# First layer's gate and up products as 2x2 blocks with seven block products

## The chip, the core and the metric

One NeuronCore of a Trainium2 chip runs the whole program. Its engines have queues of their own and work in order: TensorE (PE; weight loads are listed as PEld), VectorE (DVE), ScalarE (ACT), GpSimd (POOL) and SyncE (SP), which here only issues DMAs. The metric is the device time of one execution in microseconds (us).

## What is computed

Two layers work on 512 latent tokens x (1024 features) and 256 context tokens; the last layer keeps only the latents. Each layer has a mixer and then the FFN that the change is about, for both streams with the same weights:

```python
def swiglu(h, w_in, w_out):
    gu = h @ w_in
    return (jax.nn.silu(gu[..., :D_FF]) * gu[..., D_FF:]) @ w_out
...
x = x + mod_x[5] * swiglu(modulate(x, norm2_gain[i], mod_x[3], mod_x[4]), w_ffn_in[i], w_ffn_out[i])
...
cx = cx + mod_c[5] * swiglu(modulate(cx, norm2_gain[i], mod_c[3], mod_c[4]), w_ffn_in[i], w_ffn_out[i])
```

D_FF is 2816. All inputs are float32; `modulate` is an RMSNorm with a shift and a scale for each feature.

## The kernel before

Activations lie feature-major: 8 tiles of 128 features by the tokens, context first (columns 0 to 255), latents behind (256 to 767). Every operand of a product is split into a high part in the TensorE's float32r format and a low part, the exact rest, and a product is three matmuls: high by high, low weight by high, high weight by low (`gemm_step`, L290 to L292). A weight tile is loaded as 512 KB into one of four `rawp` buffers on SyncE's queue (`units`); ScalarE writes its high part (L272) and VectorE subtracts it for the low part (L273) into `hlp`, three buffers each.

`ffn` walks over the 22 hidden tiles j. For each it takes the gate and the up product of the context (256 columns) and of the latents (512 columns), all over 8 feature tiles k (`half`). ScalarE takes the silu of the gate out of PSUM (L883), VectorE multiplies it by the up product (L886), and `split_act` writes the high and low part of the hidden tile (L318, L319). After tiles 2, 6, 10, 14 and 18 a `chunk` takes the down products of the hidden tiles of the chunk before, two tiles in the first chunk and four in the others: for each of the 8 output tiles the context and then the latents, each in a PSUM bank of its own, and VectorE adds the result to the residual `X` (L854). The last four hidden tiles are in `finish0`.

Beside this runs `fill.tick()`, which once for each hidden tile advances the next layer's modulation vectors: a 512 KB tile of `w_mod`, two multiply-adds on VectorE (L222), and for the context two scalings on ScalarE (L219) and two adds on GpSimd (L220). The norm ahead of the FFN (`modulated`) takes the tokens' sums of squares on TensorE, a power on GpSimd (L329, `rs_n2c` and `rs_n2x`), spreads it over the partitions on TensorE and multiplies. The context's norm runs during the last products of the latents' mixer (`w_out`, names `po0x`), the latents' during the context's first gate and up products. In the latents' mixer the names are `g0x` and `b0x` for the gate and branch weights and products.

The order on each engine is that of the built program. The rows below name tiles without their numbers; the order's names keep them (`fa04` is the hidden tile 4 of layer 0).

## Time and profile before

| | |
|---|---|
| median of 3 runs | 2091.32 us (2089.07 to 2094.69) |
| span of the profiled execution | 2093.8 us |
| time of the profiled execution | no other than its span is listed |
| TensorE busy | 2024.5 us (97%) |
| VectorE, ScalarE, GpSimd busy | 1149.6, 744.4, 426.7 us (55, 36, 20%) |
| DMA, mean | 112 GB/s |

A busy time is the sum over an engine's instructions. Matmuls overlap in the records, so the start of one to the start of the next tells their rate, not their listed duration. PEclk is the clock that TensorE was granted, 1.00 for 2.4 GHz. An idle time in brackets stands in front of the instruction that ended it, with the instruction that released it.

### The profile page before, as it was taken

What the parts mean: (1) busy time and instruction counts of PE and PEld (TensorE: products, weight loads), DVE (VectorE), ACT (ScalarE), POOL (GpSimd) and SP (SyncE); (2) the same over time, 40 slices, a digit from 0 to 9 for tenths busy, and PEclk for the clock granted to TensorE, in tenths of its full rate; (3) what the DMA queues carried; (4) which work ended last, traced back from release to release, by engine and by line L of the source; (5) the groups of instructions that cost most, each with busy time, mean ns of one, the idle gap of its engine ahead of it and who ended that gap; (6) DMA issues with size and microseconds to landing.
All of it is one profiled execution on the core that took longest, in us unless ns stands there. A gap on an engine that the chain in (4) does not pass through costs nothing.

```text
span 2093.8 us, 28850 instructions
## 1 busy us (share of the span) xinstructions
PE 2024.5 (97%) x11615; PEld 1715.0 (82%) x11615; DVE 1149.6 (55%) x1765; ACT 744.4 (36%) x1231; POOL 426.7 (20%) x358
## 2 busy tenths in 40 slices
PE   7998999999899999999999999999999999999998
PEld 6988988777677888888888888787778788888887
DVE  4878638675666653434334335765756664344335
ACT  3655434344333422121313124443422333222223
POOL 4426302023664411000102013301111130000000
PEclk9999999999999999999999999999999999999999
DMA  9755633231544232222323223423336643333331
GB/s 294 207 165 153 202 101 101 63 104 51 159 153 131 81 91 73 88 81 71 91 61 101 71 71 89 109 61 90 88 102 211 178 132 91 100 95 97 101 92 59
DMA packets 326181, 233.46 MB, mean 112 GB/s; under 512 B 7648, under 2 KB 299664, under 8 KB 326048
## 3 DMA queue, kind: packets, MB, share of 16 engines
q1 hardware_dynamic: 322528, 226.78, 36.1%
q0 software_dynamic: 3280, 4.76, 1.1%
q8 instruction: 91, 1.49, 0.3%
q14 instruction: 42, 0.34, 0.0%
q10 hardware_dynamic: 240, 0.08, 0.0%
HBM read 225.30 MB, written 2.10 MB: 109 GB/s over the span
## 4 chain that ended last, share of the span: by engine, by line
PE 81%; DVE 10%; DMA 3%; issue 2%; ACT 2%; POOL 2%; ACTq 0%; SPq 0%; POOLq 0%; DVEq 0%
PE pg1x L290 2%; PE pg1x L291 2%; PE pg1x L292 2%; PE pfg0x L292 2%; PE pfg0x L291 2%; PE pfg0x L290 2%; PE pfg1x L292 2%; PE pfo0x L290 2%; PE pfo0x L291 2%; PE pfu1x L291 2%; PE pfo0x L292 2%; PE pfu1x L292 2%; PE pfu1x L290 2%; PE pfg1x L290 2%; PE pfg1x L291 2%
## 5 line engine op out<-in xcount | busy, mean ns | idle before, releaser
L220 POOL TENSOR_TENSOR mac<-mac,mq 128x512 f32<-128x512 f32 x84 | 124.4, 1481 | 296.9 <-ACT mq L219 293.0
L273 DVE TENSOR_TENSOR wl_fu<-raw_fu,wh_fu 128x1024 fp32r<-128x1024 f32 x44 | 63.6, 1446 | 153.9 <-ACT wh_fu L272 153.8
L222 DVE SCALAR_TENSOR_TENSOR mac<-wm,scv,mac 128x512 f32<-128x512 f32 x140 | 131.0, 936 | 13.4 <-DMA wm<-in_w_mod_dram 10.6
L272 ACT ACTIVATE wh_fg<-raw_fg 128x1024 fp32r<-128x1024 f32 x44 | 46.6, 1059 | 181.1 <-PE pfo0x L292 65.7
L273 DVE TENSOR_TENSOR wl_fo<-raw_fo,wh_fo 128x1024 fp32r<-128x1024 f32 x42 | 54.7, 1303 | 69.3 <-ACT wh_fo L272 69.3
L272 ACT ACTIVATE wh_fo<-raw_fo 128x1024 fp32r<-128x1024 f32 x42 | 44.4, 1058 | 122.4 <-issue 120.2
L291 PE MATMUL pg0x<-n1x0h,wl_g0x 128*128 128x512 f32 x192 | 77.2, 402 | 8.9 <-DVE wl_g0x L273 8.9
L290 PE MATMUL pg0x<-n1x0h,wh_g0x 128*128 128x512 f32 x192 | 77.1, 402 | 1.5 <-ACT wh_g0x L272 1.5
L290 PE MATMUL pg1x<-n1x1h,wh_g1x 128*128 128x512 f32 x192 | 76.4, 398 | 0.0
L292 PE MATMUL pg0x<-n1x0l,wh_g0x 128*128 128x512 f32 x192 | 76.4, 398 | 0.0
L291 PE MATMUL pg1x<-n1x1h,wl_g1x 128*128 128x512 f32 x192 | 75.8, 395 | 0.0
L292 PE MATMUL pg1x<-n1x1l,wh_g1x 128*128 128x512 f32 x192 | 75.8, 395 | 0.0
L329 POOL TENSOR_TENSOR rs_fin<-v_fin,half_neg 128x1 f32<-128x1 f32 x4 | 2.9, 721 | 355.3 <-DVE v_fin L327 355.3
L290 PE MATMUL pfg1x<-n2x1h,wh_fg 128*128 128x512 f32 (+1 forms) x184 | 70.5, 383 | 0.8 <-ACT n2x1h L359 0.8
L854 DVE SCALAR_TENSOR_TENSOR X<-pfo0x,modv,X 128x512 f32<-128x512 f32 x48 | 36.0, 750 | 64.0 <-PE pfo0x L292 64.0
L292 PE MATMUL pfg1x<-n2x1l,wh_fg 128*128 128x512 f32 (+1 forms) x184 | 70.5, 383 | 0.5 <-POOL n2x1l L360 0.3
L290 PE MATMUL pfu1x<-n2x1h,wh_fu 128*128 128x512 f32 (+1 forms) x184 | 70.0, 380 | 0.0
L291 PE MATMUL pfu1x<-n2x1h,wl_fu 128*128 128x512 f32 (+1 forms) x184 | 70.0, 380 | 0.0
L291 PE MATMUL pfg1x<-n2x1h,wl_fg 128*128 128x512 f32 (+1 forms) x184 | 69.9, 380 | 0.0
L292 PE MATMUL pfu1x<-n2x1l,wh_fu 128*128 128x512 f32 (+1 forms) x184 | 69.9, 380 | 0.0
L290 PE MATMUL pfo0x<-fa,wh_fo 128*128 128x512 f32 x176 | 69.0, 392 | 0.0
L291 PE MATMUL pfo0x<-fa,wl_fo 128*128 128x512 f32 x176 | 69.0, 392 | 0.0
(708 smaller groups left out, 6540.1 us busy)
## 6 DMA issues: line engine op xcount, KB each, us to landing
wm<-in_w_mod_dram SPq DMA_DIRECT2D x96, 512.0 KB, 4.0
raw_fg<-in_w_ffn_in_dram SPq DMA_DIRECT2D x44, 512.0 KB, 3.9
raw_fu<-in_w_ffn_in_dram SPq DMA_DIRECT2D x44, 512.0 KB, 3.8
raw_fo<-in_w_ffn_out_dram SPq DMA_DIRECT2D x42, 512.0 KB, 3.4
raw_g0c<-in_w_in_dram SPq DMA_DIRECT2D x24, 512.0 KB, 3.9
raw_g0x<-in_w_in_dram SPq DMA_DIRECT2D x24, 512.0 KB, 4.2
raw_g1x<-in_w_in_dram SPq DMA_DIRECT2D x24, 512.0 KB, 3.9
raw_wo0c<-in_w_out_dram SPq DMA_DIRECT2D x8, 512.0 KB, 4.0
```

The costliest lines, as they stand in the source:

```text
L220: G.tensor_tensor(a, a, q, ALU.add)
L222: V.scalar_tensor_tensor(a, raw[:, k, :], sck, a, ALU.mult, ALU.add)
L272: S.activation(wh, raw_ap, AF.Copy)
L273: (eng or V).tensor_tensor(wl, raw_ap, wh.bitcast(F32), ALU.subtract)
L290: T_.matmul(ps, wh, H, start=first, stop=False)
L291: T_.matmul(ps, wl, H, start=False, stop=False)
L292: T_.matmul(ps, wh, L, start=False, stop=last)
L329: G.tensor_tensor(rs, v, half_neg[:, :nb], ALU.pow)
L854: V.scalar_tensor_tensor(x, ps, modv[l][:, 40 + n, s.r:s.r + 1], x, ALU.mult, ALU.add)
```

## The change

The tokens of both streams together are cut into even and odd blocks of 128, two halves of 384 columns (one context block and two latent blocks each); the features into k tiles 0 to 3 and 4 to 7; the weights of a hidden tile into gate and up. With B for the four blocks of activations and A for the four of weights, a hidden tile's gate and up for both halves come from seven products of 4 k tiles by 384 columns instead of the eight that the blocks have: A11 B11, A12 B21, S1 T1, S2 T2, S3 T3, S4 B22, A22 T4 in the names of the code, where S and T are sums of weight blocks and of activation blocks. Sums of the products are made partly in PSUM, by products that are added into the same bank, and partly on VectorE.

The T sums are made once (`combine`); the S sums for every hidden tile from the loaded weights (`sums`, on GpSimd for tiles 0 and 1, on VectorE for the others), and the split is of S2, S1, S3, S4 and of A11, A12, A22. `Pipeline` prepares items (two products each, the last of a tile one; or two output tiles of a chunk) ahead of the products. The activations' norm is made by halves (`norm`); the last three `w_out` tiles of the latents are taken by halves, too, and half 0 is normed during the products of half 1 (`last_first`). In `chunk` the context and the latents share a PSUM tile (columns 512 to 767 and 0 to 511). Tiles 0 to 2 are interleaved at the start.

The raw buffers are five instead of four, for the whole kernel. Keys, attention and activation buffers lie in zones that are closed and opened by stage, so that the seven pairs of B and T blocks have room. Layer 1's FFN is as before.

```diff
-    rawp = ctx.enter_context(tc.tile_pool(name="rawp", bufs=4))
+    rawp = ctx.enter_context(tc.tile_pool(name="rawp", bufs=5))
     hlp = ctx.enter_context(tc.tile_pool(name="hlp", bufs=3))
-    act = ctx.enter_context(tc.tile_pool(name="act", bufs=11))
...
+    def zone(name, bufs, side="left"):
+        zones[name] = ExitStack()
+        return zones[name].enter_context(tc.tile_pool(name=name, bufs=bufs, side=side, reuse_waits="tile"))
...
+            ps = pmain(f"po{nm0}{n}_{a}{st.name}")[:, :st.T]
+            if st.odd is not None:
+                p3 = ps.rearrange("p (b t) -> p b t", t=P)
+                gemm(p3, ws[n], KT, *[[blocks(y, st.odd) for y in x] for x in yo])
+                x = blocks(X[:, n, s.cols], st.odd)
+                V.scalar_tensor_tensor(x, p3, modv[l][:, 16 + n, s.r:s.r + 1], x, ALU.mult, ALU.add)
+                q = t2(f"sq{st.name}{n}", st.T)
+                S.activation(q.rearrange("p (b t) -> p b t", t=P), x, AF.Square)
+                if n == KT - 1:
+                    acc.append(q)
+                else:
+                    t = blocks(acc[0], st.odd)
+                    G.tensor_tensor(t, t, q.rearrange("p (b t) -> p b t", t=P), ALU.add)
+                return
...
+        def split(self, nm, src, k0, k1):
+            c = self.C[nm]
+            S.activation(c[:, 0, k0:k1, :], src, AF.Copy)
+            V.tensor_tensor(c[:, 1, k0:k1, :], src, c[:, 0, k0:k1, :].bitcast(F32), ALU.subtract)
...
+        def norm(self, i, ss):
+            l = self.l
+            rs = rstd(ss(), 2, f"n2h{i}", D)
+            yield
+            rb = ps_s.tile([P, 1024], F32, tag="ps", name=f"ps_rbh{i}")[:, :HT]
...
+            for k in range(KT):
+                y = t[k // 4][:, k % 4, :]
+                V.tensor_tensor(y.rearrange("p (b t) -> p b t", t=P), blocks(X[:, k, :], i), rb.rearrange("p (b t) -> p b t", t=P), ALU.mult)
+                a, b = A2[l], modv[l]
+                S.activation(y[:, :P], y[:, :P], AF.Identity, bias=b[:, 24 + k, 1:2], scale=a[:, k, 1:2])
+                if k % 2:
+                    S.activation(y[:, P:], y[:, P:], AF.Identity, bias=b[:, 24 + k, 0:1], scale=a[:, k, 0:1])
+                else:
+                    V.tensor_scalar(y[:, P:], y[:, P:], a[:, k, 0:1], b[:, 24 + k, 0:1], ALU.mult, ALU.add)
+                yield
...
+            b11, b21, b12, b22 = self.t
+            T2 = self.fap.tile([P, 4, HT], F32, tag="fa", name="T2")
+            self.combo("T2")
+            for h in (slice(0, 2), slice(2, 4)):
+                V.tensor_tensor(b11[:, h], b12[:, h], b11[:, h], ALU.subtract)
+                V.tensor_tensor(T2[:, h], b22[:, h], b11[:, h], ALU.subtract)
+                self.split("T2", T2[:, h], h.start, h.stop)
+                yield
+            self.combo("T1")
+            self.split("T1", b11, 0, 4)
+            yield
+            V.tensor_tensor(b12, b22, b12, ALU.subtract)
+            self.combo("T3")
+            self.split("T3", b12, 0, 4)
+            yield
+            self.combo("B22")
+            self.split("B22", b22, 0, 4)
+            yield
+            V.tensor_tensor(b21, b21, T2, ALU.subtract)
+            self.combo("T4")
+            self.split("T4", b21, 0, 4)
...
+        def product(self, ps, w, k0, nm, first):
+            c = self.C[nm]
+            wh, wl = w
+            for k in range(4):
+                H, L = c[:, 0, k, :], c[:, 1, k, :]
+                T_.matmul(ps, wh[:, k0 + k, :], H, start=first and k == 0, stop=False, skip_group_check=True)
+                T_.matmul(ps, wl[:, k0 + k, :], H, start=False, stop=False, skip_group_check=True)
+                T_.matmul(ps, wh[:, k0 + k, :], L, start=False, stop=k == 3, skip_group_check=True)
...
+            def sums(which, eng=V):
+                g, u = d["g"], d["u"]
+                a11, a12, a21, a22 = g[:, 0:4, :], g[:, 4:8, :], u[:, 0:4, :], u[:, 4:8, :]
+                for x in which:
+                    if x == 3:
+                        d["S3"] = self.sp.tile([P, 4, P], F32, tag="S3", name=f"S3{j}")
+                        eng.tensor_tensor(d["S3"], a11, a21, ALU.subtract)
+                    elif x == 1:
+                        eng.tensor_tensor(a21, a21, a22, ALU.add)
+                    elif x == 2:
+                        eng.tensor_tensor(a11, a21, a11, ALU.subtract)
+                    else:
+                        eng.tensor_tensor(a12, a12, a11, ALU.subtract)
...
+            def prep_a():
+                load()
+                if early is None:
+                    sums((3, 1))
+                w = parts("sg", d["g"])
+                if early is None:
+                    sums((2,))
+                elif early < 2:
+                    sums((3, 1, 2, 4), G)
+                return w
+            def prep_b():
+                if early == 2:
+                    sums((3, 1, 2))
+                w = parts("sb", d["g"][:, 0:4, :], d["u"][:, 0:4, :])
+                if early in (None, 2):
+                    sums((4,))
+                return w
+            def prep_c():
+                return parts("sc", d["S3"], d["g"][:, 4:8, :])
+            def prep_d():
+                return parts("su", d["u"][:, 4:8, :])
...
+                self.product(d["P"], w, 0, "B11", True)
+                if early is None:
+                    evac_m()
+                elif early == 0:
+                    next(self.nx)
+                self.product(d["Q"], w, 4, "B21", True)
+                if early is None:
+                    evac_g()
+                else:
+                    self.late.append((evac_m, evac_g))
...
+            def evac_g():
+                d["g1"] = t2(f"g1{j}", HT)
+                V.tensor_tensor(d["g1"], d["Q"], d["m"], ALU.add)
+                S.activation(d["g1"], d["g1"], AF.Silu)
+            def run_b(w):
+                self.product(d["P"], w, 0, "T2", False)
+                d["m6"] = t2(f"m6{j}", HT)
+                S.activation(d["m6"], d["P"], AF.Copy)
+                d["R"] = bank(f"pR{j}") if early != 1 else ps_s.tile([P, 1024], F32, tag="ps", name=f"pR{j}")[:, :HT]
+                self.product(d["R"], w, 4, "T1", True)
+                d["m5"] = t2(f"m5{j}", HT)
+                S.activation(d["m5"], d["R"], AF.Copy)
+            def run_c(w):
+                self.product(d["P"], w, 0, "T3", False)
+                V.tensor_tensor(d["m5"], d["P"], d["m5"], ALU.add)
+                self.product(d["R"], w, 4, "B22", False)
+                V.tensor_tensor(d["m6"], d["R"], d["m6"], ALU.add)
+                S.activation(d["m6"], d["m6"], AF.Silu)
+            def run_d(w):
+                self.product(d["P"], w, 0, "T4", False)
+                H, L = A(j)
+                for i, (x, y) in enumerate(((d["P"], d["g1"]), (d["m5"], d["m6"]))):
+                    V.tensor_tensor(y, x, y, ALU.mult)
+                    y3 = y.rearrange("p (b t) -> p b t", t=P)
+                    S.activation(blocks(H, i), y3, AF.Copy)
+                    V.tensor_tensor(blocks(L, i), y3, blocks(H, i).bitcast(F32), ALU.subtract)
+                fill.tick()
...
+                def go(w, n=n):
+                    for i in range(2):
+                        ps = ps_s.tile([P, 1024], F32, tag="ps", name=f"pfo{l}{c0}{n + i}")
+                        for s in streams:
+                            o = 512 if s.r else 0
+                            down(s, n + i, [x[:, :, i * P:(i + 1) * P] for x in w], c0, m, ps[:, o:o + s.T])
...
+            p = [sv.pair(j, hidden, j) for j in range(3)]
+            for j, x in ((0, 0), (1, 0), (2, 0), (0, 1), (1, 1), (0, 2), (1, 2), (0, 3), (1, 3), (2, 1), (2, 2), (2, 3)):
+                yield p[j][x]
+                if j == 2 and x == 3:
+                    yield from chunk(0)
+            for j in range(3, NF):
+                yield from sv.pair(j, hidden)
+                if j in heads:
+                    yield from chunk(heads[heads.index(j) - 1])
...
+    seven = Seven(0)
+    def last_first(one, acc):
+        for i in range(2):
+            st = Stream(f"x{'eo'[i]}", CTX, 256, 0)
+            st.odd = i
+            part = [acc[0]]
+            acc0.append(part)
+            for n in range(KT - 3, KT):
+                one(n, st, part)
+                fill.tick()
+                if i:
+                    steps(n0, {KT - 3: 2, KT - 2: 4, KT - 1: 3}[n])
+            if i == 0:
+                close("att", "kkp")
+                seven.fap = zone("fap", 6, "right")
+                half_ss(0)
+                n0 = seven.norm(0, lambda: ssh[0])
+                next(n0)
...
+    pipe, end = ffn_seven(seven, [SC, SX], 0, finish0, [mod_steps(1, 0, 4)])
+    half_ss(1)
+    seven.nx = seven.norm(1, lambda: ssh[1])
+    for x, nm in enumerate(("B11", "B21")):
+        seven.combo(nm)
+        for h in (0, 2):
+            seven.split(nm, seven.t[x][:, h:h + 2, :], h, h + 2)
+        if x == 0:
+            pipe.fill(1)
+            next(seven.nx)
+    pipe.fill(2)
+    for _ in range(3):
+        pipe.step()
+    run(seven.nx)
+    cm = seven.combine()
+    seven.late[0][0]()
+    steps(cm, 2)
+    for m, _ in seven.late[1:]:
+        m()
+    for _, g in seven.late:
+        g()
+    run(cm)
+    while pipe.step():
+        pass
+    close("sp", "cbp")
+    open_act()
+    end()
```

GpSimd between the latents' mixer and the FFN, before: adds of squares (`sq_m0x`), the two streams' low parts (`n2c0l`, `n2x0l`) and the power for the latents (`rs_n2x`).

```order
L372 TENSOR_TENSOR sq_m0x0_6494<-sq_m0x0_6494,sq_m0x5_6702 128x512
L372 TENSOR_TENSOR sq_m0x0_6494<-sq_m0x0_6494,sq_m0x6_6742 128x512
L360 TENSOR_TENSOR n2c0l0_6544<-t_n2c05_6745,n2c0h0_6543 128x256
L329 TENSOR_TENSOR rs_n2x0_6845<-v_n2x0_6843,half_neg_97 128x4
L360 TENSOR_TENSOR n2c0l0_6544<-t_n2c07_6789,n2c0h0_6543 128x256
L360 TENSOR_TENSOR n2x0l0_6882<-t_n2x01_6889,n2x0h0_6880 128x512
L360 TENSOR_TENSOR n2x0l0_6882<-t_n2x03_6899,n2x0h0_6880 128x512
```

GpSimd at the same place now; `rs_n2h1` is the power for half 1, `raw_u0` and `raw_g0` the sums S1 and S2 in place.

```order
L859 TENSOR_TENSOR sq_m0x0_6509<-sq_m0x0_6509,sqxo6_6833 128x2x128
L1098 TENSOR_TENSOR S30_6910<-raw_g00_6902,raw_u00_6904 128x512
L1098 TENSOR_TENSOR S31_6932<-raw_g01_6924,raw_u01_6926 128x512
L1100 TENSOR_TENSOR raw_u00_6904<-raw_u00_6904 128x512
L1100 TENSOR_TENSOR raw_u01_6926<-raw_u01_6926 128x512
L1102 TENSOR_TENSOR raw_g00_6902<-raw_u00_6904,raw_g00_6902 128x512
L360 TENSOR_TENSOR rs_n2h1_6917<-v_n2h1_6915,half_neg_93 128x2
```

Five weight sums stand between the last add of squares and the power; the low parts have left the engine. On TensorE the matmuls that spread this power, `ps_rbh1`, stand ahead of the first product of tile 0, `pP0`.

VectorE during one hidden tile (4) before:

```order
L886 TENSOR_TENSOR sg0c4_7566<-sg0c4_7566,pfu0c4_7568 128x256
L319 TENSOR_TENSOR fa04_7528<-sg0c4_7566,fa04_7528 128x256
L273 TENSOR_TENSOR wl_fu02_384_7661<-raw_fu02_384_7658,wh_fu02_384_7660 128x1024
L886 TENSOR_TENSOR sg0x4_7621<-sg0x4_7621,pfu0x4_7623 128x512
L273 TENSOR_TENSOR wl_fg06_0_7800<-raw_fg06_0_7797,wh_fg06_0_7799 128x1024
L319 TENSOR_TENSOR fa04_7528<-sg0x4_7621,fa04_7528 128x512
```

VectorE during one hidden tile now; `m5`, `m6` and `g1` are sums of products, `raw_g05` and `raw_u05` hold the next tile's weights:

```order
L1104 TENSOR_TENSOR raw_g05_7777<-raw_g05_7777 128x512
L1190 TENSOR_TENSOR m64_7760<-pR4_7762,m64_7760 128x384
L1113 TENSOR_TENSOR wl_sb5_7817<-raw_g05_7777,wh_sb5_7816 128x512
L1113 TENSOR_TENSOR wl_sb5_7817<-raw_u05_7779,wh_sb5_7816 128x512
L1197 TENSOR_TENSOR m64_7760<-m54_7775,m64_7760 128x384
L1197 TENSOR_TENSOR g14_7741<-pP4_7713,g14_7741 128x384
L1113 TENSOR_TENSOR wl_sc5_7843<-S35_7781,wh_sc5_7842 128x512
L1200 TENSOR_TENSOR fa04_7835<-m64_7760,fa04_7835 128x3x128
L1113 TENSOR_TENSOR wl_sc5_7843<-raw_g05_7777,wh_sc5_7842 128x512
L1200 TENSOR_TENSOR fa04_7835<-g14_7741,fa04_7835 128x3x128
L1174 TENSOR_TENSOR g15_7876<-pS5_7849,m5_7862 128x384
L1113 TENSOR_TENSOR wl_su5_7880<-raw_u05_7779,wh_su5_7879 128x512
```

Six instructions for a tile became seventeen, and the next tile's sums and splits lie between this tile's sums out of PSUM; S3 and S1 of the tile after that stand further ahead.

VectorE at the start of a four-tile chunk before (down weights `fo`, hidden tile 6, first updates of `X`):

```order
L886 TENSOR_TENSOR sg0x6_7889<-sg0x6_7889,pfu0x6_7891 128x512
L273 TENSOR_TENSOR wl_fo02_512_8056<-raw_fo02_512_8053,wh_fo02_512_8055 128x1024
L319 TENSOR_TENSOR fa06_7796<-sg0x6_7889,fa06_7796 128x512
L854 SCALAR_TENSOR_TENSOR X_117<-pfo0c20_0_7935,modv0_134,X_117 128x256
L854 SCALAR_TENSOR_TENSOR X_117<-pfo0x20_0_7949,modv0_134,X_117 128x512
L854 SCALAR_TENSOR_TENSOR X_117<-pfo0c21_0_7963,modv0_134,X_117 128x256
```

VectorE at the start of the same chunk now:

```order
L1197 TENSOR_TENSOR g16_8033<-pP6_8005,g16_8033 128x384
L1197 TENSOR_TENSOR m66_8052<-m56_8067,m66_8052 128x384
L304 TENSOR_TENSOR wl_fo024_8140<-raw_fo024_8137,wh_fo024_8139 128x1024
L1200 TENSOR_TENSOR fa06_8120<-g16_8033,fa06_8120 128x3x128
L1200 TENSOR_TENSOR fa06_8120<-m66_8052,fa06_8120 128x3x128
L1221 SCALAR_TENSOR_TENSOR X_113<-pfo020_8143,modv0_141,X_113 128x256
L1221 SCALAR_TENSOR_TENSOR X_113<-pfo021_8170,modv0_141,X_113 128x256
L1098 TENSOR_TENSOR S37_8261<-raw_g07_8257,raw_u07_8259 128x512
L1100 TENSOR_TENSOR raw_u07_8259<-raw_u07_8259 128x512
L1098 TENSOR_TENSOR S38_8458<-raw_g08_8454,raw_u08_8456 128x512
L1100 TENSOR_TENSOR raw_u08_8456<-raw_u08_8456 128x512
L1221 SCALAR_TENSOR_TENSOR X_113<-pfo020_8143,modv0_141,X_113 128x512
```

Splits, both low halves of tile 6 and then the context's updates stand ahead, and S3 and S1 of tiles 7 and 8 ahead of the latents' updates.

## Rows read from the trace of the kernel before

**Rows 1.** Head of the page: span, then busy time of each engine.
```profile
span 2093.8 us, 28850 instructions
...
PE 2024.5 (97%) x11615; PEld 1715.0 (82%) x11615; DVE 1149.6 (55%) x1765; ACT 744.4 (36%) x1231; POOL 426.7 (20%) x358
```

**Rows 2.** Table by stretch, three stretches; first line gives the columns.
```profile
core 0: us, PE busy (x) PEld busy (x) DVE busy (x) ACT busy (x) POOL busy (x), PEclk, DMA share, GB/s
...
332.00:660.00 328.00, 308.29 (x1715) 243.42 (x1714) 222.23 (x360) 137.45 (x246) 127.65 (x94) 0.97 0.37 107
...
711.00:733.00 22.00, 21.16 (x139) 18.96 (x138) 14.81 (x27) 13.65 (x22) 9.52 (x7) 1.00 0.17 51
733.00:1238.00 505.00, 504.68 (x2939) 444.19 (x2938) 206.45 (x265) 120.81 (x174) 41.15 (x30) 1.00 0.27 81
```

**Rows 3.** Timeline of TensorE, gate products: start, duration, line, operation.
```profile
900.11 0.28 PE L291 MATMUL pfg0c<-n2c0h,wl_fg 128*128 128x256 f32 x1
...
900.83 0.28 PE L291 MATMUL pfg0c<-n2c0h,wl_fg 128*128 128x256 f32 x1
...
907.82 0.39 PE L290 MATMUL pfg0x<-n2x0h,wh_fg 128*128 128x512 f32 x1
...
908.50 0.39 PE L290 MATMUL pfg0x<-n2x0h,wh_fg 128*128 128x512 f32 x1
```

**Rows 4.** Groups by line and shape, VectorE, 660 to 1264 us: busy, mean ns.
```profile
L273 DVE TENSOR_TENSOR wl_fu<-raw_fu,wh_fu 128x1024 fp32r<-128x1024 f32 x22 | 36.6, 1666 | 89.2 <-ACT wh_fu L272 89.0
...
L273 DVE TENSOR_TENSOR wl_fg<-raw_fg,wh_fg 128x1024 fp32r<-128x1024 f32 x22 | 27.1, 1232 | 6.6 <-ACT wh_fg L272 6.6
L222 DVE SCALAR_TENSOR_TENSOR mac<-wm,scv,mac 128x512 f32<-128x512 f32 x28 | 22.0, 785 | 7.7 <-DMA wm<-in_w_mod_dram 7.1
L854 DVE SCALAR_TENSOR_TENSOR X<-pfo0c,modv,X 128x256 f32<-128x256 f32 x44 | 21.2, 481 | 12.7 <-PE pfo0c L292 12.5
L319 DVE TENSOR_TENSOR fa<-sg0x,fa 128x512 fp32r<-128x512 f32 x22 | 18.4, 834 | 0.0
L886 DVE TENSOR_TENSOR sg0x<-sg0x,pfu0x 128x512 f32<-128x512 f32 x22 | 15.1, 688 | 33.4 <-PE pfu0x L292 33.4
...
L886 DVE TENSOR_TENSOR sg0c<-sg0c,pfu0c 128x256 f32<-128x256 f32 x22 | 9.3, 421 | 53.6 <-PE pfu0c L292 53.6
...
L360 DVE TENSOR_TENSOR n2x0l<-t_n2x,n2x0h 128x512 fp32r<-128x512 f32 x4 | 2.8, 703 | 0.4 <-ACT n2x0h L359 0.4
```

**Rows 5.** Timeline around 762 us: GpSimd's row and VectorE's row.
```profile
761.22 2.67 POOL L220 TENSOR_TENSOR mac<-mac,mq 128x512 f32<-128x512 f32 x2 [16.50 <-ACT mq L219]
...
762.67 2.30 DVE L273 TENSOR_TENSOR wl_fo<-raw_fo,wh_fo 128x1024 fp32r<-128x1024 f32 x1 [6.87 <-ACT wh_fo L272]
```

**Rows 6.** Groups by line and shape, GpSimd, 660 to 1264 us.
```profile
L372 POOL TENSOR_TENSOR sq_m0x<-sq_m0x,sq_m0x 128x512 f32<-128x512 f32 x6 | 10.1, 1686 | 20.4 <-ACT sq_m0x L368 20.4
...
L360 POOL TENSOR_TENSOR n2x0l<-t_n2x,n2x0h 128x512 fp32r<-128x512 f32 x4 | 5.2, 1302 | 8.0 <-ACT n2x0h L359 8.0
...
L329 POOL TENSOR_TENSOR rs_n2c<-v_n2c,half_neg 128x2 f32<-128x2 f32 x1 | 0.7, 725 | 3.0 <-DVE v_n2c L327 3.0
```

**Rows 7.** Timeline of TensorE after a wait; in brackets the idle and its releaser.
```profile
641.18 0.79 PE L291 MATMUL pb0x<-y00xh,wl_b0x 128*128 128x512 f32 x1 [4.72 <-DVE wl_b0x L273]
...
645.61 0.60 PE L292 MATMUL pb0x<-y00xl,wh_b0x 128*128 128x512 f32 x1
646.04 0.40 PE L290 MATMUL pg0x<-n1x0h,wh_g0x 128*128 128x512 f32 x1
646.28 0.39 PE L291 MATMUL pg0x<-n1x0h,wl_g0x 128*128 128x512 f32 x1
```

**Rows 8.** Waits of TensorE and of ScalarE: total us, times, longest us.
```profile
PE pg0x L291 <- DVE wl_g0x L273: 8.9, 3, 4.8
...
ACT wh_g0x L272 <- DMA raw_g0x<-in_w_in_dram: 45.0, 10, 7.2
```

**Rows 9.** Timeline of VectorE ahead of that wait.
```profile
631.84 7.56 DVE L222 SCALAR_TENSOR_TENSOR mac<-wm,scv,mac 128x512 f32<-128x512 f32 x6
```

More of the change, by code (lines that the diff above doesn't have):

```diff
@@ L1 @@
 import math
+from collections import deque
 from contextlib import ExitStack
@@ L41, in __init__ @@
         self.NB = T // P
+        self.odd = None
     @property
@@ L941, in ffn, with __init__, fill, step @@
         chunk(heads[-1])
+    class Pipeline:
+        def __init__(self, items, depth):
+            self.items, self.depth, self.ready = iter(items), depth, deque()
+        def fill(self, n=None):
+            while len(self.ready) < (self.depth + 1 if n is None else n):
+                item = next(self.items, None)
+                if item is None:
+                    return
+                self.ready.append((item[1], item[0]()))
+        def step(self):
+            self.fill()
+            if not self.ready:
+                return False
+            do, w = self.ready.popleft()
+            do(w)
+            return True
```

139 lines of the change are left out of this document (128 added, 11 removed).

## The prediction

> **What bounds the kernel now.** I read the page's head first, then the table of stretches, then single rows. The profiled execution spans 2093.8 us and TensorE is busy for 2024.5 us of it; VectorE follows with 55% [rows 1]. The page shows no time outside the span, so the sum below is made against 2093.8 us; the median of the runs, 2091.32 us, is 2.5 us lower. The table by stretch shows where TensorE's idle time lies. In the first layer's FFN (733 to 1238 us) it idles 0.3 us of 505, and 0.84 us in the norm ahead of it (711 to 733). In the latents' mixer (332 to 660) it idles 19.7 of 328 us at a granted clock of 0.97 [rows 2]. So in the FFN a matmul saved is time saved, and nothing else is there to gain; any new wait of TensorE is a loss at full price. VectorE is busy 206 of the 505 us there, ScalarE 121: that is the room in which the scheme's sums must fit.
>
> **TensorE's work.** Three 512-column matmuls take from 907.82 to 908.50, one every 0.227 us; six of 256 columns from 900.11 to 900.83, one every 0.120 us [rows 3]. Both are 0.417 ns a column and 13 ns fixed, so the 384-column matmul, which the trace does not show at this depth, is taken at 0.173 us; its bounds are the two rows around it, and a break between them is not in sight. A hidden tile has 48 matmuls of each width (8 k x 3 x gate and up): 48 x 0.120 + 48 x 0.227 = 16.64 us. After: 7 products x 4 k x 3 = 84 x 0.173 = 14.56 us. 22 tiles: **-45.8 us**. The down products keep their 48 matmuls a tile. Three w_out tiles of the latents become two 256-column halves: 3 x 24 x (2 x 0.120 - 0.227) = **+1.0 us**.
> The Trainium skill ("TensorE: Matmul & The Clock Gate", Back-to-back issue gap) states N/2.4 + 2.5 ns; by it, as an estimate, a tile would save 1.95 us and all of them 42.9. The rows show some 11 ns more for each matmul than it states, so the measurement decides.
>
> **VectorE's work for a tile.** Before: two 1024-element splits (1.23 and 1.67), two products out of PSUM (0.42 and 0.69) and two low halves (the context's taken like its product, 0.42, the latents' 0.83), 5.3 us [rows 4]. After, 17 instructions: four sums of weights and five splits of 512 (0.70 each, the row of n2x0l: 6.3), one split of 1024 (1.23), and five sums or products out of PSUM and two low halves of 384, between the 0.42 of 256 and the 0.69 of 512 columns, so 0.555 each (3.9): 11.4 us. Two steps of a modulation sum add 2 x 0.785. That is 13.0 of the 14.56 us that TensorE needs for the tile; before, it was under half. It hides as long as nothing makes the queue wait. Two things do. S3 and S1 of a later tile stand in VectorE's queue ahead of this tile's sums and wait for a load (the order of VectorE shows it); and VectorE slows beside GpSimd: a 1024-element split took 2.30 us while GpSimd added two modulation rows (2.67 us) [rows 5], and wl_fg 1.23 in the mean [rows 4], so +1.07 us. GpSimd adds two rows a tile.
> The Trainium skill ("GPSIMD Engine Reference", Key points) says that GpSimd shares its SBUF interfaces with VectorE and contends with instructions that have two SBUF inputs. The trace agrees [rows 5], and the sums of weights and the splits are all such instructions, so this rule speaks against the change; its price in the sum is the 1.07 us of the row.
> With those 1.07 us a tile needs 14.1 us of VectorE, 0.5 less than TensorE. The 19 tiles in the steady rhythm then wait now and then; bounds are 0 and 1.2 us a tile (1.07 and a load that is late once more), and I take 0.4: **+8 us** (0 to 23), nearer to the margin that is left than to the full collision.
>
> **The transition.** Before, the latents' norm runs beside the context's first products, and TensorE idles 0.84 us in all [rows 2]. After, the first product needs both streams, and only half 0 is normed during w_out. I replayed the built program's order with the durations of the rows. (a) The factor of half 1 is a power on GpSimd, queued behind five weight sums; TensorE's two matmuls of it stand ahead of the first product, in the same queue. By the replay GpSimd's last add of squares ends 1.6 us after w_out; five sums of 1.30 (the row of n2x0l) to 1.69 us (the row of sq_m0x) and the power (0.73) follow [rows 6]: 8.8 to 10.7 us, less 0.5 for the matmuls of the squares: 9 us idle. (b) After an idle 4.72 us the rows show matmuls at 0.43 us for 4.9 us, TensorE's lower clock of 1.2 GHz, then 0.23 again [rows 7]: 2.4 us lost. (c) B11 and B21 for tiles 0 to 2 are six products, 12.5 us. In these VectorE must norm half 1 (eight of 0.555 and four more), make b11, T2 and its split and two splits of weights; T2 comes some 4.3 us late, and the clock falls again, 2.4. (d) T1, T3, B22 and T4 follow one another on VectorE, with a split of 1536 elements each (1.8 us by the slope of 0.70 for 512 and 1.23 for 1024) and a sum. TensorE's 14 products (29 us) end 18.9 us late by the replay, 0.8 more than (a) to (c). (e) Tile 2's T4 waits for the m5 sum, 4 us, and the first chunk for its updates of X, 5 us. Sum 9 + 2.4 + 4.3 + 2.4 + 0.8 + 4 + 5 = **+28 us** (20 to 36).
>
> **The down chunks.** The two streams' products of a tile now share one PSUM tile, so the latents' matmuls wait until X has taken the context's (0.48 us [rows 4]). They had banks of their own. Within a chunk the next tile's context product, 1.4 us, covers that. At the start of the four later chunks VectorE still holds splits, both low halves, and S3 and S1 of the next tiles, which wait for loads: 2 us each, **+8** (2 to 16). The end, with its own tiles from a reopened zone, +1.5 (0 to 4).
>
> **The fifth raw buffer** is there for the whole kernel. In the latents' mixer ScalarE waited 45.0 us for raw_g0x loads in ten waits, and TensorE 8.9 us for the splits behind them [rows 8]; elsewhere VectorE ran six modulation steps in a row, 7.56 us [rows 9], ahead of the split for which TensorE idled 4.72 us [rows 7]. A load that starts one buffer earlier can take some of the 19.7 us away; the order of these instructions is almost unchanged. Bounds 0 and -18; I take -6, since bunched steps on VectorE remain.
>
> **Sum.** -45.8 + 1.0 + 8 + 28 + 8 + 1.5 - 6 = -5.3: 2088.5 us of span, 2086 us beside the median.
>
> **Rivals.**
> 1. Clean gain. The replay is too dark: the weight sums on GpSimd start before the last add of squares or run at 1.30, T2 is in time, and the rhythm is covered. Then the transition is 12, the tiles 4, the chunks 4: -45.8 + 1 + 12 + 4 + 4 + 1 - 6 = -30, so 2061 us. For it: VectorE needs 13.0 of 14.56 us and items are prepared three ahead. Against: the power stands five sums back.
> 2. Slower: VectorE becomes the bound in the tiles. It decides once a tile needs over 14.56 us of VectorE, waits included. At 15.8 (the row's collision and one late load in each) TensorE loses 1.2 x 19 = 23 us and each chunk starts on a longer queue, 4 us instead of 2 (16): -45.8 + 1 + 23 + 28 + 16 + 1.5 - 6 = +18, so 2109 us. For it: in the mixer, where VectorE is busy 68%, TensorE idles 6% [rows 2]; here it would be 88 to 97%. Against: 58 us of block products for four tiles are followed by 33 us of down products with little for VectorE.
> 3. The buffer does the most: the forecast with -18 in the mixer, 2074 us.
>
> **How the numbers follow.** The forecast's case, 2074 to 2098, has 0.45; rival 1 0.22, rival 2 0.22, rival 3 0.11. About 0.3% (6.3 us) can be told from no change: faster is under 2085.0, slower over 2097.6. The forecast's case gives 0.20 faster, 0.21 same, 0.04 slower; rivals 1 and 3 are faster, rival 2 slower but for 0.04: faster 0.53, same 0.25, slower 0.22. The predicted time lies just inside "same", since the forecast's case straddles the bound and two rivals stand below it. The range takes in all but the outer part of rivals 1 and 2: 2058 to 2110.
>
> **What would show it.** In the profile after: pP matmuls starting every 0.173 us and TensorE's busy time about 45 us lower; an idle of some 9 us ahead of ps_rbh1, released by GpSimd's power, and one of some 4 us ahead of pP0 with T2, each followed by a granted clock near one half; short idles of pP, pS and pR released by VectorE; at the head of each chunk the latents' pfo0 released by X; the latents' mixer shorter than its 328 us. The forecast is wrong if the rhythm holds without idles (then rival 1), if VectorE has no idle time left in the tiles (rival 2), or if the 384-column matmuls do not start every 0.173 us.

## The result, and the profile after

The kernel after takes **2111.64 us** (median of 4 runs, 2110.22 to 2115.96) against 2090.6 us of before (2089.07 to 2094.69): the ratio is 1.0103, interval 1.0088 to 1.0118. It is 1.0% slower. The forecast was 2086.0, in a range that ended at 2110. The profiled execution spans 2108.2 us, 14.4 more than before; the sum of the prediction had -5.3.

The head of the page after, to be read beside [rows 1]:

```profile
span 2108.2 us, 28931 instructions
...
PE 2014.7 (96%) x11423; PEld 1721.2 (82%) x11423; DVE 1287.2 (61%) x2014; ACT 820.5 (39%) x1400; POOL 444.7 (21%) x361
```

192 matmuls fewer took TensorE only 9.8 us fewer. The table by stretch after, with the columns of [rows 2]:

```profile
332.00:660.00 328.00, 320.90 (x1779) 252.05 (x1778) 231.39 (x369) 142.21 (x253) 132.86 (x96) 0.99 0.38 113
...
711.00:733.00 22.00, 18.41 (x87) 17.85 (x88) 17.78 (x29) 14.21 (x26) 5.55 (x4) 0.81 0.01 1
733.00:1238.00 505.00, 479.72 (x2693) 450.32 (x2692) 333.27 (x502) 189.00 (x325) 51.22 (x32) 0.98 0.28 84
```

In the mixer TensorE idles 7.1 us where it idled 19.7; in the FFN it idles 25.3 of 505 us where it idled 0.3, at a granted clock of 0.98, and of 0.81 in the stretch around the first wait. What it waits for there, from the table of waits (total us, times, longest):

```profile
PE pP L1077 <- DVE m L1188: 12.1, 7, 2.9
PE pfo L321 <- DVE X L1221: 9.5, 7, 3.4
PE ps_rbh L1033 <- POOL rs_n2h L360: 9.0, 1, 9.0
...
PE pP L1077 <- ACT cbT L1022: 2.9, 1, 2.9
```

The first is T4's product behind the sum `m5`, which takes T3's product out of the same bank, the second the latents' down product behind the context's update of `X`, the third the power behind the weight sums, the fourth T2. All four stood in the prediction. GpSimd's timeline (start, duration) shows the third:

```profile
700.66 3.47 POOL L1098 TENSOR_TENSOR S<-raw_g,raw_u 128x512 f32<-128x512 f32 x2
704.09 4.19 POOL L1100 TENSOR_TENSOR raw_u<-raw_u 128x512 f32<-128x512 f32 x2
708.24 1.97 POOL L1102 TENSOR_TENSOR raw_g<-raw_u,raw_g 128x512 f32<-128x512 f32 x1
710.18 1.42 POOL L360 TENSOR_TENSOR rs_n2h<-v_n2h,half_neg 128x2 f32<-128x2 f32 x1
```

Nothing in this explains the rest of the kernel. I split the span at TensorE's first and last `pg0x` and its last `pfo0x` (mixer, FFN with the w_out ahead of it, tail up to the end), all in us:

| kernel | mixer | FFN | tail |
|---|---|---|---|
| before | 328.0 | 600.3 | 833.2 |
| after | 314.5 | 615.3 | 845.0 |

The tail, mostly layer 1, is computed as before by the same matmuls, and took 11.8 us more. One timeline of TensorE in layer 1's FFN, before and after (each pair: the first and the 52nd start behind it):

```profile
1800.06 0.39 PE L291 MATMUL pfg1x<-n2x1h,wl_fg 128*128 128x512 f32 x1
...
1811.84 0.39 PE L292 MATMUL pfg1x<-n2x1l,wh_fg 128*128 128x512 f32 x1
```
```profile
1809.66 0.39 PE L322 MATMUL pfg1x<-n2x1h,wl_fg 128*128 128x512 f32 x1
...
1821.79 0.39 PE L323 MATMUL pfu1x<-n2x1l,wh_fu 128*128 128x512 f32 x1
```

11.78 / 52 = 0.2265 us before, 12.13 / 52 = 0.2333 us after, without idle time and at the full clock in both. The same instruction became 3% slower. That was the first question.

### The profile page after: what moved, and what is told of

Same layout as the page of the kernel before. It is cut to its first block, busy times and chain, and to the rows that moved or that the text cites. A ratio compares the mean times of both kernels' runs of the same rounds, so it can differ in the third digit from the quotient of the medians.

```text
span 2108.2 us, 28931 instructions
## 1 busy us (share of the span) xinstructions
PE 2014.7 (96%) x11423; PEld 1721.2 (82%) x11423; DVE 1287.2 (61%) x2014; ACT 820.5 (39%) x1400; POOL 444.7 (21%) x361
## 4 chain that ended last, share of the span: by engine, by line
PE 76%; DVE 13%; DMA 4%; issue 3%; ACT 3%; POOL 1%; ACTq 0%; POOLq 0%; DVEq 0%; SPq 0%
PE pfo L321 2%; PE pfo L323 2%; PE pP L1077 2%; PE pfo L322 2%; PE pP L1078 2%; PE pP L1079 2%; PE pfg1x L323 2%; PE pg1x L321 2%; PE pfu1x L323 2%; PE pfu1x L322 2%; PE pfu1x L321 2%; PE pfg1x L321 2%; PE pfg1x L322 2%; PE pg1x L322 2%; PE pg1x L323 2%
## 5 line engine op out<-in xcount | busy, mean ns | idle before, releaser
L251 POOL TENSOR_TENSOR mac<-mac,mq 128x512 f32<-128x512 f32 x84 | 133.6, 1590 | 270.5 <-ACT mq L250 266.8
L253 DVE SCALAR_TENSOR_TENSOR mac<-wm,scv,mac 128x512 f32<-128x512 f32 x140 | 132.4, 945 | 11.6 <-DMA wm<-in_w_mod_dram 9.3
L321 PE MATMUL pfo<-fa,wh_fo 128*128 128x512 f32 (+1 forms) x288 | 99.4, 348 | 9.7 <-DVE X L1221 9.5
L323 PE MATMUL pfo<-fa,wh_fo 128*128 128x512 f32 (+1 forms) x288 | 97.2, 338 | 0.0
L322 PE MATMUL pfo<-fa,wl_fo 128*128 128x512 f32 (+1 forms) x288 | 97.1, 337 | 0.0
L303 ACT ACTIVATE wh_fo<-raw_fo 128x1024 fp32r<-128x1024 f32 (+1 forms) x44 | 44.8, 1019 | 115.3 <-issue 111.2
L1221 DVE SCALAR_TENSOR_TENSOR X<-pfo,modv,X 128x256 f32<-128x256 f32 (+1 forms) x80 | 48.1, 614 | 62.2 <-PE pfo L323 61.8
L304 DVE TENSOR_TENSOR wl_fo<-raw_fo,wh_fo 128x1024 fp32r<-128x1024 f32 (+1 forms) x44 | 53.7, 1222 | 47.6 <-ACT wh_fo L303 47.4
L321 PEld LDWEIGHTS pfo<-fa,wh_fo 128*128 128x128 f32 x288 | 54.3, 189 | 19.8 <-DVE X L1221 13.2
```

The source lines that it names most:

```text
L251: G.tensor_tensor(a, a, q, ALU.add)
L253: V.scalar_tensor_tensor(a, raw[:, k, :], sck, a, ALU.mult, ALU.add)
L303: S.activation(wh, raw_ap, AF.Copy)
L304: (eng or V).tensor_tensor(wl, raw_ap, wh.bitcast(F32), ALU.subtract)
L321: T_.matmul(ps, wh, H, start=first, stop=False)
L322: T_.matmul(ps, wl, H, start=False, stop=False)
```

## The experiments: where the time came from

What the new pools did to these matmuls is move their operands. By the addresses in the built programs, counted in bytes within a partition modulo 512, before has every weight tile and every moving tile but attention's keys at 352; after has weights at 416 and moving tiles at 288 (layer 0's hidden tiles `fa` mostly at 480). Four kernels ask whether that is it. The first shifts after's tiles back into step, the second puts before's out of step, the third gives before only the fifth raw buffer:

after_aligned (the left pad of 128 bytes moves the activations from 288 to 416, the right-hand pad of 64 the hidden tiles and the keys from 480 to 416; the weights stay at 416):
```diff
+    padrp = ctx.enter_context(tc.tile_pool(name="padrp", bufs=1, side="right"))
+    padr = padrp.tile([P, 16], F32, name="padr")
+    V.memset(padr, 0.0)
+    padap = ctx.enter_context(tc.tile_pool(name="padap", bufs=1))
+    pada = padap.tile([P, 32], F32, name="pada")
+    V.memset(pada, 0.0)
```


> The changed kernel with two unused paddings, 128 bytes a partition ahead of the activation zone and 64 bytes at the right end, so that weights and moving activations start at the same byte modulo 512 (416 and 416), as in the kernel before (352 and 352); in the changed kernel they are 416 and 288, and 416 and 480 for the hidden tiles. Theory (the layout sets the matmuls' rate): 512-column matmuls start every 0.227 us again instead of 0.232, and the time falls by some 24 us to about 2088 us. Rival (the rate was that of the run or comes with the new work): rate and time stay, 2108 to 2114 us.

before_shift (weights 352, moving tiles 224; the smaller DMA scratch makes room):
```diff
+    padap = ctx.enter_context(tc.tile_pool(name="padap", bufs=1))
+    pada = padap.tile([P, 96], F32, name="pada")
+    V.memset(pada, 0.0)
...
+    nc = bacc.Bacc("TRN2", ..., dynamic_dma_scratch_size=12288)
```


> The kernel before with an unused padding of 384 bytes a partition between weights and activations, so that moving activations start 128 bytes below the weights modulo 512 (224 and 352), as in the changed kernel; nothing else is changed but the DMA scratch, made smaller to give the room. Theory (layout): 512-column matmuls start every 0.232 us instead of 0.227, 256-column ones every 0.1185 instead of 0.120, over the whole program, some 27 us: about 2117 us. Rival: no change, 2090 us.

before_raw5:
```diff
-    rawp = ctx.enter_context(tc.tile_pool(name="rawp", bufs=4))
+    rawp = ctx.enter_context(tc.tile_pool(name="rawp", bufs=5))
...
+    nc = bacc.Bacc("TRN2", ..., dynamic_dma_scratch_size=4096)
```


> The kernel before with five raw buffers instead of four (4096 bytes, so the layout modulo 512 is unchanged). Theory (the fifth buffer shortened the latents' mixer in the changed kernel, from 328 to 315 us in spite of slower matmuls): TensorE's idle time there falls from 19 to about 7 us and the program takes about 2074 us. Rival (zones or the changed end of the mixer did it): 2088 to 2092 us.

cadence_grid is only matmuls: blocks of 24 (8 k, high by high, low weight by high, high weight by low) at 8 x 8 places of weights and moving operand, 64 bytes apart; everything else of the layer is left out.
```python
for k in range(8):
    T_.matmul(ps, WH[:, b], H[:, a], start=(k == 0), stop=False)
    T_.matmul(ps, WL[:, b], H[:, a], start=False, stop=False)
    T_.matmul(ps, WH[:, b], L[:, a], start=False, stop=(k == 7))
```


> Only matmuls of the kernel's form (high by high, low by high, high by low, eight k tiles), all other work and the result left out: blocks of 24 with weights and moving activations at eight byte residues modulo 512 each, in steps of 64, no other engine busy. Theory (layout): the time from start to start of 512 columns is near 0.227 us at residues 352 and 352, 0.232 at 416 (weights) and 288 (activations), 0.229 at 416 and 480, and depends on the difference of the two. Rival: the same for all.

**Measured.** Ratios to before, with 95% intervals, for these and for all kernels below:

| kernel | median us (range, runs) | ratio |
|---|---|---|
| after_aligned | 2088.35 (2084.39 to 2092.74, 10) | 0.9990 [0.9979, 1.0002] |
| before_shift | 2117.77 (2115.13 to 2119.37, 4) | 1.0128 [1.0112, 1.0145] |
| before_raw5 | 2076.73 (2075.73 to 2080.55, 4) | 0.9938 [0.9918, 0.9958] |
| fix_power | 2087.59 (2083.51 to 2091.70, 10) | 0.9981 [0.9970, 0.9993] |
| fix_sum | 2087.53 (2085.21 to 2088.14, 10) | 0.9983 [0.9972, 0.9994] |
| fix_bank | 2074.13 (2072.91 to 2078.55, 4) | 0.9926 [0.9910, 0.9942] |
| fix_all | 2070.56 (2070.31 to 2073.16, 4) | 0.9908 [0.9893, 0.9923] |
| mods_chunks | 2065.82 (2064.91 to 2067.57, 4) | 0.9886 [0.9870, 0.9903] |
| power_bank_mods | 2064.19 (2063.61 to 2066.91, 4) | 0.9883 [0.9868, 0.9897] |
| all_mods | 2065.27 (2061.97 to 2067.30, 4) | 0.9884 [0.9869, 0.9898] |
| mods_noload | 2062.85 (2061.42 to 2067.64, 4) | 0.9869 [0.9850, 0.9888] |

The first three kernels were timed together, the four fix kernels together, the next three together and mods_noload by itself. Each ratio is to before as it was timed beside them; before's median went from 2088.7 to 2091.4 us, so 1 to 3 us between medians of different groups can come from that alone.

192 bytes of padding take 23.3 us from the kernel after; 384 bytes of it cost the kernel before some 26. Layer 1's matmuls in after_aligned and in before_shift, the same rows as above:

```profile
1799.92 0.39 PE L328 MATMUL pfg1x<-n2x1h,wl_fg 128*128 128x512 f32 x1
...
1811.70 0.39 PE L329 MATMUL pfu1x<-n2x1l,wh_fu 128*128 128x512 f32 x1
```
```profile
1824.77 0.39 PE L294 MATMUL pfg1x<-n2x1h,wl_fg 128*128 128x512 f32 x1
...
1836.90 0.39 PE L295 MATMUL pfg1x<-n2x1l,wh_fg 128*128 128x512 f32 x1
```

They start every 0.2265 and every 0.2333 us: the pace follows the padding and not the kernel. The tails are 831.6 us in after_aligned and 845.0 in after. The grid says what of the place counts; here the blocks with both operands at 352, and with the moving one at 288 and the weights at 416, as in after (in a block's name the first of the last two letters is the moving operand's place, the second the weights'):

```profile
184.38 0.39 PE L69 MATMUL mdd<-H,WH 128*128 128x512 f32 x1
...
189.61 0.39 PE L71 MATMUL mdd<-L,WH 128*128 128x512 f32 x1
```
```profile
145.57 0.39 PE L69 MATMUL mce<-H,WH 128*128 128x512 f32 x1
...
150.91 0.39 PE L71 MATMUL mce<-L,WH 128*128 128x512 f32 x1
```

5.23 / 23 = 0.2274 us against 5.34 / 23 = 0.2322. Over the 64 places (the first block, which was interrupted, left out) the interval depends on the difference alone, moving place less weight place, modulo 256 bytes: 227.4 ns in the mean at 0, 229.3 at 64, 232.3 at 128, 233.4 at 192. After stands at 128 for most tiles and at 64 for the `fa` at 480. In the whole kernels the step from 0 to 128 is somewhat larger than in the grid, 226.7 to 233.3 ns in the mean of layer 1's gate and up products; why is open.

**What the layout does not explain.** before_raw5 takes 14.7 us off before, and its mixer is 311.8 us for 328.0; TensorE idles 9.7 us there for 19.7, in the columns of [rows 2]:

```profile
332.00:660.00 328.00, 318.29 (x1789) 253.40 (x1788) 231.67 (x367) 142.14 (x253) 133.00 (x97) 0.99 0.38 113
```

So before_raw5 is the fair partner of after_aligned, with the same buffers and the same pace: the scheme by itself goes from 2076.7 to 2088.4, **+11.6 us**, and the FFN from 599.0 to 610.5. The block products start every 0.176 us in after (0.174 in the mean in after_aligned), as the timeline of one half tile after shows, 23 intervals in 4.05 us:

```profile
808.28 0.34 PE L1077 MATMUL pP<-cbB,wh_sg 128*128 128x384 f32 x1
...
812.33 0.34 PE L1079 MATMUL pS<-cbB,wh_sg 128*128 128x384 f32 x1
```

So the 45 us of matmuls are saved, and 57 us are given back inside the FFN. In after_aligned TensorE idles 21.5 us in the transition (counted up to 782 us, with the first waits of the first chunk) and 15.6 behind it. The granted clock fell to one half in four stretches of the transition and three behind it; the matmuls that started late in them cost 7.3 and 5.0 us. One of the three, in the columns of [rows 2]:

```profile
921.17:924.50 3.33, 3.33 (x10) 3.33 (x11) 3.33 (x6) 1.56 (x3) 0.00 (x0) 0.51 0.00 0
```

Ten matmuls took 3.33 us where ten take 1.74 at the full clock. The three stretches stand behind the longest waits, of 2.6 to 2.9 us; behind the other waits there, of up to 1.4 us, the granted clock stayed at 1.00 and some 0.1 us was lost each time. The profiled execution of after_aligned was the longest of its ten, so these figures may be at the upper end. The next kernels, all on after_aligned, take single causes away.

## The experiments: the waits inside the FFN

fix_power lets the weight sums of tiles 0 and 1 come behind the power on GpSimd:
```diff
-            rs = rstd(ss(), 2, f"n2h{i}", D)
+            rs = self.rs1 = rstd(ss(), 2, f"n2h{i}", D)
...
-                elif early < 2:
-                    sums((3, 1, 2, 4), G)
...
+                elif early is not None:
+                    sums((3, 1, 2, 4), G)
...
+                        if eng is G:
+                            G.tensor_tensor(d["S3"][:, 0, 0:2], self.rs1, half_neg[:, :2], ALU.mult)
```


> after_aligned, with the weight sums of tiles 0 and 1 held back on GpSimd until the power of half 1 is done (a two-element GpSimd write into their buffer that reads the power comes first). Theory (the power queued behind five sums costs the idle of 9.0 us ahead of ps_rbh and the slow clock behind it): the idle falls to 1 to 2 us, some 9 us less in all, 2079 us. Rival (VectorE, busy 9.7 of 10 us there, is what bounds the transition): T2 comes as late as before, the idle moves to pP with T2, gain under 3 us, 2085 to 2090.

fix_sum lets ScalarE take T3's product out of PSUM, so that TensorE's next product need not wait for VectorE:
```diff
-                V.tensor_tensor(d["m5"], d["P"], d["m5"], ALU.add)
+                m3 = t2(f"m3{j}", HT)
+                S.activation(m3, d["P"], AF.Copy)
+                V.tensor_tensor(d["m5"], m3, d["m5"], ALU.add)
```


> after_aligned, with the bank of T2 and T3 copied out by ScalarE ahead of T4, so that T4's matmuls wait for ScalarE's copy and VectorE adds later from the copy (one more ScalarE instruction of 0.49 us and a buffer for each tile). Theory (T4 waits because VectorE's sum out of PSUM stands behind a 1.2 us split in its queue): the waits of pP for VectorE's m, 10 us in after_aligned, and the lower clock behind five of them vanish, some 12 us, 2076 us. Rival (VectorE as a whole is too busy in the tiles): the waits come back at splits or at the next tile, gain under 4 us.

fix_bank gives the context's down product a PSUM bank of its own again:
```diff
-                            o = 512 if s.r else 0
-                            down(..., ps[:, o:o + s.T])
+                            pc = ps_y.tile([P, 512], F32, tag="py", ...) if s.r else ps
+                            down(..., pc[:, :s.T])
```


> after_aligned, with the context's down products in a PSUM bank of their own, so that the latents' do not wait for X to take them. Theory (the shared PSUM tile makes the waits at the head of the chunks): the waits of pfo for X, 9.4 us in after_aligned, fall to 1 or 2, and with the clock some 8 us, 2080 us. Rival (VectorE comes late to X in any case): the single context bank is waited for instead, gain under 3 us.

fix_all has the three together.


> The three together. If the causes are separate, their gains add up: some 29 us, 2060 us, 16 under the kernel before with five buffers (2076.7). If VectorE as a whole is the bound, no more than the largest of the three.

**Measured.** fix_power and fix_sum are 0.8 us from after_aligned, too little to tell from nothing where single runs lie 4 us to either side; both times came as the rivals had them. Their waits show why; fix_power first:

```profile
PE pP L1083 <- DVE m L1196: 10.1, 6, 2.9
PE pfo L327 <- DVE X L1229: 9.3, 5, 3.4
PE pP L1083 <- ACT cbT L1028: 7.6, 1, 7.6
...
PE ps_rbh L1039 <- POOL rs_n2h L366: 2.0, 1, 2.0
```
```profile
PE pfo L327 <- DVE X L1229: 12.0, 6, 4.3
...
PE pP L1083 <- ACT m L1176: 5.3, 5, 1.3
```

With the power early, its wait falls from 9.0 us to 2.0, and the wait for T2 rises from 3.0 to 7.6: T2 was late by the norm of half 1 on VectorE and ScalarE as well, and most of the idle time ahead of the power only lay in front of it. The two together fall from 12.0 to 9.6 us, so 2 to 3 us are left as the power's own. fix_sum's ten microseconds moved to ScalarE's copies (5.3), to `X` (9.6 in after_aligned, 12.0 here) and to single waits for other VectorE work (3.0). Both waits belong to chains that are late by more than the step that was moved.

fix_bank takes 14.2 us. The wait of `pfo` for `X` is gone (2.8 us of `pfoc` remain), the idle behind the transition falls from 15.6 to 11.4 us, and of the three stretches at the lower clock there one is left. And TensorE's change from the context's to the latents' matmuls is itself shorter. The timeline of after_aligned:

```profile
866.81 0.28 PE L329 MATMUL pfo<-fa,wh_fo 128*128 128x256 f32 x1
867.07 0.50 PE L327 MATMUL pfo<-fa,wh_fo 128*128 128x512 f32 x1
867.41 0.39 PE L328 MATMUL pfo<-fa,wl_fo 128*128 128x512 f32 x1
```

and that of fix_bank:

```profile
863.35 0.28 PE L329 MATMUL pfoc<-fa,wh_fo 128*128 128x256 f32 x1
863.47 0.40 PE L327 MATMUL pfo<-fa,wh_fo 128*128 128x512 f32 x1
863.70 0.40 PE L328 MATMUL pfo<-fa,wl_fo 128*128 128x512 f32 x1
```

0.60 us for two steps against 0.35, no idle marked in either; over two output tiles 8.60 against 8.36 us, 0.24 less in each of some 20 pairs, an estimated 4.8 us. The order on TensorE is another, too: after_aligned takes the context of two output tiles and then the latents of both, fix_bank changes after each tile.

fix_all, with the power and the copy added, is 3.6 us under fix_bank and 17.8 under after_aligned, and not the 29 us that its theory had.

In fix_bank `pP` still waits 10.9 us for `m5`. Its VectorE does not lack time; it waits for a load. The rows from the waits of TensorE, of VectorE and of SyncE's queue in fix_bank, the last two from 782 to 1242 us:

```profile
PE pP L1083 <- DVE m L1194: 10.9, 8, 2.9
...
DVE S L1104 <- DMA raw_u<-in_w_ffn_in_dram: 33.0, 13, 3.8
...
SPq L1096 <- DVE wl_sc L1119: 135.9, 9, 24.3
```

and one of VectorE's 13 in its timeline, S3 and then `m5`, with the matmul of TensorE that waits for `m5`:

```profile
1103.73 1.05 DVE L1104 TENSOR_TENSOR S<-raw_g,raw_u 128x512 f32<-128x512 f32 x1 [2.24 <-DMA raw_u<-in_w_ffn_in_dram]
1104.70 1.21 DVE L1119 TENSOR_TENSOR wl_sg<-raw_g,wh_sg 128x1024 fp32r<-128x1024 f32 x1
1105.84 0.55 DVE L1194 TENSOR_TENSOR m<-pP,m 128x384 f32<-128x384 f32 x1
...
1106.44 0.44 PE L1083 MATMUL pP<-cbT,wh_su 128*128 128x384 f32 x1 [2.92 <-DVE m L1194]
```

A tile's gate buffer (`raw_g`) is held until `wl_sc` has read it, SyncE's queue waits for that, and the modulation steps use buffers of the same pool in the same tiles. Two kernels take that apart. mods_chunks is fix_bank with the modulation steps moved from the tiles into the down chunks:
```diff
-                fill.tick()
+                if j >= NF - 2:
+                    fill.tick()
...
                             down(..., pc[:, :s.T])
+                    fill.tick()
```


> fix_bank, with the next layer's modulation steps taken beside the down products instead of once a tile (the last two tiles keep theirs). In fix_bank VectorE waits 33 us in the first FFN for raw_u loads ahead of S3, and SyncE's queue waits 136 us for buffers that wl_sc frees. Theory (in the tiles VectorE is not too busy but held by loads for which no raw buffer is free): with one load less in each tile the waits for raw_u fall under 12 us, the waits of pP for VectorE's m from 10.9 us to under 3, and the time by some 10 us to about 2064 us. Rival (VectorE's own work bounds the tiles): 1.6 us less of it a tile brings the same waits down by under half, 2070 us or more. Rival (the steps only move): new waits of pfo for X take it back, 2074 us.

mods_noload is fix_bank with the modulation steps where they were, but reading a resident tile: the loads of layer 1's first four modulation pieces, and with them their true values, are left out.
```diff
+                if l == 1 and u < 4:
+                    v = vtm.rearrange("p b d -> p (b d)")[:, 0:512]
+                    raw = v.unsqueeze(1).to_broadcast([P, 2, 512])
+                else:
                     raw = rawp.tile([P, 2, 512], F32, tag="raw", ...)
                     nc.sync.dma_start(raw, ...)
```


> fix_bank, with the loads of the next layer's first four modulation tiles left out: the same VectorE, ScalarE and GpSimd steps, once a tile, read a buffer that is there already (so the result is not the layer's). Theory (in the tiles VectorE is held by loads that find no raw buffer free): the waits of pP for VectorE's m fall from 10.9 to under 4 us and the time to some 2066 us, as with the steps moved. Rival (it is VectorE's and GpSimd's work in the tile): those waits stay over 8 us, 2072 us or more.

**Measured.** mods_chunks takes 8.3 us more off fix_bank, mods_noload 11.3. In the waits of VectorE the line above becomes, in mods_chunks and in mods_noload:

```profile
DVE S L1104 <- DMA raw_u<-in_w_ffn_in_dram: 18.5, 11, 3.7
```
```profile
DVE S L1108 <- DMA raw_u<-in_w_ffn_in_dram: 12.3, 12, 3.2
```

mods_noload leaves every step of VectorE and GpSimd in the tiles and gains the whole: it was the loads, not the work on what they load. From 782 to 1242 us VectorE was busy 298.9 us in fix_bank and 300.2 in mods_noload (the third busy time in the columns of [rows 2]):

```profile
782.00:1242.00 460.00, 448.63 (x2580) 422.72 (x2580) 298.91 (x455) 174.05 (x298) 52.34 (x33) 1.00 0.27 83
```
```profile
782.00:1242.00 460.00, 454.82 (x2644) 430.41 (x2643) 300.18 (x454) 179.40 (x308) 57.36 (x39) 0.99 0.23 69
```

Leaving a load out spares its buffer and its transfer. For the buffer speak the 135.9 us that SyncE's queue waited for `wl_sc`, with the DMA engines busy 27% of the time; no run separates the two. TensorE's wait of `pP` for `m5` falls from 10.9 us to 4.2 in mods_noload and to 0.2 in mods_chunks, where a wait at the chunks takes part of its place:

```profile
PE pP L1087 <- DVE m L1198: 4.2, 2, 3.1
```
```profile
PE pfoc L327 <- DVE X L1228: 8.1, 6, 2.0
```

The times came as the theory had them or better, two of its signs did not quite: VectorE's waits for `raw_u` in mods_chunks fell to 18.5 us and not under 12, and TensorE's for `m5` in mods_noload to 4.2 and not under 4.

power_bank_mods is mods_chunks with fix_power, all_mods has fix_sum too.


> mods_chunks with the weight sums of tiles 0 and 1 behind the power, as in fix_power. Theory (the transition's chain runs through VectorE and ScalarE to T2): the idle at ps_rbh falls from 9 to 2 us and the one ahead of T2 grows from 3 to 7.5, so 1 to 3 us less than mods_chunks. Rival (the power is the cause): 8 us less.

> power_bank_mods with ScalarE's copy ahead of T4, as in fix_sum. If T4's waits came from loads, the copy has nothing left to give and costs ScalarE's time: within 2 us of power_bank_mods. If VectorE's queue is still late, 4 us less.

They agree with mods_chunks to 1.6 and 0.6 us, within the spread of their runs: the power is worth at most the 1 to 3 us that were expected here, the copy on ScalarE nothing that can be told. power_bank_mods at 2064.19 us is the fastest version of the true computation, 1.2% below before; but 14.7 us of that are the fifth buffer's, which before could have without the scheme. The scheme as such, at its best here, brings 2076.7 - 2064.2 = 12.5 us of the 45 that its matmuls save (11.5 by the ratios of the table).

## Why the prediction was wrong, step by step

- **The layout, +23.3 us, was not in the sum at all.** The step that failed is the one that took the pace of [rows 3] for the kernel after: matmuls that the change does not touch stood in the sum at nothing, and of the new pools only the fifth buffer had a term. The runs showed that the pools moved the operands, and that the 512-column matmul starts every 233.3 ns in place of 226.7. after_aligned (-23.3), before_shift (+26) and the grid show it; without this term the forecast of 2086.0 stands 2.4 us beside after_aligned's 2088.35. That agreement is partly two errors that cancel, as follows.
- **Matmuls -45.8: right.** The 384-column matmul, which no row had shown, started every 0.174 us in the mean in after_aligned and every 0.176 in after.
- **The transition +28: right in sum,** 21.5 idle and 7.3 at the lower clock, 28.8 us. Its parts (a), 9.0 us, and (c), 2.9 for 4.3, came as told; of (e) T4 of tile 2 came to 0.6 us for 4, the first chunk to 3.4 for 5. But (a) and (c) were no separate causes: fix_power shows one chain, the norm of half 1 up to T2, that stays late by 9.6 of their 12.0 us.
- **Tiles and chunks +16, end +1.5: too small.** 15.6 us of idle, 5.0 at the lower clock and an estimated 4.8 at the changes of PSUM region are some 25, for 17.5. The waits are those named (`m5` behind S3, which waits for a load; the latents' matmuls behind `X`). What was left out is that the clock fell behind the three longest of these waits; the transition counted it, in (b) and (c), the tiles and chunks did not. The change of region was not thought of.
- **The fifth buffer -6: right in mechanism, too small.** -14.7 us by before_raw5, near the bound of 18 that [rows 8, 9] gave; the likely value was put too near to the middle.
- **The rivals.** The time is nearest to rival 2, 2109, but not by its mechanism. VectorE was busy 333 of 505 us (66%); it waited for loads that came late, and mods_noload gave 11.3 us back with all of VectorE's work in place. Its collision with GpSimd is real all the same, as the last section shows. Rival 3 (the buffer does most) is right on the buffer and lost to the layout. Rival 1's rhythm with few idles came about only in the repaired kernels (6.3 us behind the transition in mods_chunks).

Open: how much of what is left in the chunks of mods_chunks is contention with GpSimd and how much the order of VectorE's queue; and whether a sixth raw buffer would do what mods_noload does, which no run shows.

## What to carry to other kernels

A change that moves buffers is also a change of every matmul's operands: compare the pace of matmuls that the change does not touch before explaining the ones that it does. When a wait is taken away and the time stays, look for the wait that grew by as much; only fix_bank and the loads gave back more than the runs' spread here, and two plausible repairs did not. A tile that several stages share (a PSUM pair, a raw buffer) is held until its last reader, so ask of each new reader what load or product stands behind it.
